# Splitting the branch weights ahead of the first gate product in three merges of a two-layer diffusion block

## The chip, the cores and the metric

The kernel runs on one core of a Trainium2 chip. The metric is device time in microseconds (us), median of several executions. A profile is one execution with the hardware profiler; its rows are quoted below. PE is TensorE, DVE is VectorE, ACT is ScalarE, POOL is GpSimd, SP the queue that issues most transfers.

## What is computed

Two layers over 256 latent tokens (x) and, in layer 0 only, 256 context tokens as well. Each layer has a normalised input projection, three parallel mixers (attention, convolution, pooling), a merge of them with gates, and then 16 routed experts whose weights are streamed from memory. The part that matters here:

```
y_a = attn @ w_attn_o;  y_b = conv(..) @ w_conv_o;  y_c = pool(..) @ w_pool_o
g_a, g_b, g_c = split(sigmoid(gate_in), 3)          # gate_in: 3 x 1024 columns of h @ w_in
out = (g_a * y_a + g_b * y_b + g_c * y_c) @ w_out
```

## The kernel before

**Split products.** Every product of the layer body is made of three fast products. `split` (L229 to L240) turns 128x1024 weights into a high half, written by ACT (L238), and a low half, the weights minus the high half, written by DVE or POOL (L239). Both halves go into one tile `ws`. `mm3` then multiplies: first the high half with both halves of the activations (L496 and L497 in turn, two for each of `nk` blocks), then the low half with the high activations (L499, one for each block). So a product can start when ACT is done, and needs the low half only two thirds later. Which engine makes the low half is in the table `LOW`: a letter for each layer, v for DVE and p for POOL (`g0="vv"`, `g1="pv"`, `g2="vp"`, `wo="vv"`).

**The `ws` buffers.** Tiles `ws` come from a pool with two buffers. In layer 1 (`last`), every third split takes a third buffer of its own (pool `DR`). A tile is released when its last reader is done. The framework has a scheduler that orders the instructions of each engine at build time, by a priority that follows the order of the code and by when a buffer comes free; `split` lifts its two instructions ahead by a fixed amount (`SPLIT_PRIO`). On the chip each engine works through its own list in order.

**A merge.** `merge(bi, w_o, brt)` runs three times in each layer: branch 0 (attention, L763), branch 2 (pooling, L811), branch 1 (convolution, L820). It walks four column blocks q. A q has two steps v. A step has a gate product (`unit`, called u0 or u1 here by its v: 24 matmuls against `hh`, `hl`), a tanh on ACT, and a branch product (p0, p1: 12 matmuls against `br`, `brp` or `brc`), which DVE then multiplies with the gate; POOL adds it to the sum in branches 2 and 1 (L761). The gate weights of u0 and u1 are split apart (called g0 and g1 here); the branch weights are split once for both steps of a q (called wo here). In layer 0 a matmul has 512 columns, in layer 1 it has 256.

**What else is woven in.** The convolution's taps (L478) run on DVE under the first merge. `pump_mod` puts 4 modulation products (L255, for the next stage) behind a unit, `mod_group` ends with `modr` on DVE (L264), transposes (L271) and one product (L294). The scheduler may move all of these. Weight tiles `w` come through a ring of five buffers filled by SP.

Of the kernel before, what the change touches and what calls it, by code (L numbers as in the profile page):

```python
# [27 lines left out]
LOW = dict(q="vv", k="pv", v="pv", cg="vv", ca="vv", pu="pv", g0="vv", g1="pv", g2="vp", wo="vv", wout="pv")  # L28
# [99 lines left out]
def dit_block(ctx: ExitStack, tc: tile.TileContext, out, kcv, kb16, rope_in, tok, cols, w_mod0, w_mod,  # L128
# [16 lines left out]
    def bank(tag, dt=F32):  # L145
        pool, bufs = psum[tag]
        return pool.tile([128, 512], dt, tag=tag, name=tag, bufs=bufs)
# [19 lines left out]
    def t2(name, n=512, dt=F32):  # L167
        return L.tile([128, n], dt, tag="t2", name=name, bufs=6)
# [42 lines left out]
    for l in range(DEPTH):  # L211
# [10 lines left out]
        def load(src, view, **kw):  # L222
            t = ring()
            nc.sync.dma_start(t, src)
            return t.rearrange(view, **kw)
# [3 lines left out]
        def split(src, view, eng="v", **kw):  # L229
            nsplit[0] += 1  # L230
            if last and nsplit[0] % 3 == 0 and not tail[0]:
                w = DR.tile([128, 2048], F32R, tag="ws", name="ws")
            else:
                w = LW["pool"].tile([128, 2048], F32R, tag="ws", name="ws", bufs=2)
            hi, lo = w[:, :1024], w[:, 1024:]
            h, lw = hi.rearrange(view, **kw), lo.rearrange(view, **kw)
            with tc.high_priority(SPLIT_PRIO[l]):
                nc.scalar.activation(h, src, AF.Copy)  # L238
                (nc.gpsimd if eng == "p" else nc.vector).tensor_sub(lw, src, h.bitcast(F32))  # L239
            return hi, lo  # L240
# [126 lines left out]
        for s in range(2):  # L367
# [8 lines left out]
            for t in range(2):  # L376
                nc.vector.tensor_scalar(xn[s][:, t, :], XS[s][:, t, :], r[:, t:t + 1],
                                        None, op0=ALU.mult)
# [91 lines left out]
        def pump_taps(n):  # L470
            for _ in range(min(n, len(taps))):
                ch, k = taps.popleft()
                if k == 0:
                    nc.vector.tensor_scalar(acc[:, ch], up[:, ch, :, 0:256], dw[:, ch:ch + 1],
                                            vec[:, VCB + 4 * l + ch:VCB + 4 * l + ch + 1],
                                            op0=ALU.mult, op1=ALU.add)
                else:
                    nc.vector.scalar_tensor_tensor(acc[:, ch], up[:, ch, :, k:k + 256],  # L478
                                                   dw[:, 4 * k + ch:4 * k + ch + 1], acc[:, ch],
                                                   op0=ALU.mult, op1=ALU.add)  # L480
# [11 lines left out]
        def mm3(ps, w, a, nk, n):  # L492

            (wh, wl), (ah, al) = w, a
            for k in range(nk):
                nc.tensor.matmul(ps, wh[:, k, :], ah[:, k, :n], start=k == 0, stop=False)  # L496
                nc.tensor.matmul(ps, wh[:, k, :], al[:, k, :n], start=False, stop=False)  # L497
            for k in range(nk):
                nc.tensor.matmul(ps, wl[:, k, :], ah[:, k, :n], start=False, stop=k == nk - 1)  # L499

        def unit(src, n, view="p (k n) -> p k n", eng="v", **kw):
            w = split(src, view, eng, **(kw or dict(k=8)))
            w = [v.rearrange("p (k n) -> p k n", k=8) for v in w]
            ps = bank("mm")
            mm3(ps[:, :n], w, (hh, hl), 8, n)
            nunit[0] += 1
            if nunit[0] % MOD_EVERY[l] == 0:
                pump_mod()
            return ps

        def win(c0):
            return load(w_in[l, c0 // 256], "p (k n) -> p k n", k=8)
# [224 lines left out]
        def merge(bi, w_o, brt, fill=None):  # L737
            for q in range(4):
                if q % 2 == 0:
                    wo = load(w_o[l, q // 2], "p (k n) -> p k n", k=4)  # L740
                wgt = win(OGATE + 1024 * bi + 256 * q)
                ws = None
                for v in range(2):
                    j = 2 * q + v
                    pg = unit(wgt[:, :, 128 * v:128 * v + 128], N, eng=LOW[f"g{bi}"][l])
                    th = t2("th", N)
                    nc.scalar.activation(th, pg[:, :N], AF.Tanh, scale=0.5)
                    if ws is None:
                        ws = split(wo[:, :, 256 * (q % 2):256 * (q % 2) + 256], "p (k n) -> p k n",
                                   LOW["wo"][l], k=4)  # L750
                        ws = [z.rearrange("p (k n) -> p k n", k=4) for z in ws]
                    py = bank("mm")
                    mm3(py[:, :N], [z[:, :, 128 * v:128 * v + 128] for z in ws],
                        (brt[:, 0], brt[:, 1]), 4, N)
                    if bi == 0:
                        nc.vector.scalar_tensor_tensor(m[j], th, 1.0, py[:, :N], op0=ALU.add,
                                                       op1=ALU.mult)
                    else:
                        nc.vector.scalar_tensor_tensor(th, th, 1.0, py[:, :N], op0=ALU.add,
                                                       op1=ALU.mult)  # L760
                        nc.gpsimd.tensor_add(m[j], m[j], th)  # L761
                    pump_taps(TAPS.get(f"merge{bi}", (0, 0))[l])
                    if fill is not None and not taps:  # L763
                        next(fill, None)

        merge(0, w_attn_o, br)

        brp = branch("brp")
# [40 lines left out]

        cn = conv_norm()  # L810
        merge(2, w_pool_o, brp, cn)  # L811
        pump_taps(len(taps))
        for _ in cn:
            pass
        brc = branch("brc")
        for ch in range(4):
            z = acc[:, ch].rearrange("p s n -> p (s n)")
            nc.scalar.activation(brc[:, 0, ch, :], z, AF.Copy)
            nc.vector.tensor_sub(brc[:, 1, ch, :], z, brc[:, 0, ch, :].bitcast(F32))
        merge(1, w_conv_o, brc)  # L820
        pump_mod(100)

# [210 lines left out]
        for e in range(NE):  # L1033
# [36 lines left out]
            for i in range(4):  # L1070
                wg, wu = [eload().rearrange("p (k n) -> p k n", k=2) for _ in range(2)]
                for kk in range(2):
                    k = 2 * i + kk
# [126 lines left out]
```

## Time and profile before

| | us |
|---|---|
| median of 3 executions | 1696.55 (1694.93 to 1698.94) |
| the profiled execution | 1699.61 |
| its span, first to last instruction | 1697.8 |

PE is busy for 1469.8 us, 87% of the span; DVE for 40%, ACT for 24%, POOL for 14%. By time, the merges of layer 0 take 201 to 425 us, those of layer 1 take 1080 to 1205 us, and the experts follow each. A row of a timeline gives start, length, engine, line, operation, output and input, then in brackets how long the engine was idle before it and what ended that. The ends of matmuls are modelled, so the distance of two starts is the better measure of a matmul.

### The profile page before, as it was taken

Reading aid. Unit: us, or ns where it says so; the run is one execution under the profiler, and the core shown is the slowest. Engines: PE = TensorE matmul, PEld = TensorE weight load, DVE = VectorE, ACT = ScalarE, POOL = GpSimd, SP = SyncE. Lnnn points to the kernel's source line nnn. Section 1 sums busy time; section 2 is a strip of 40 time slices with the busy share of each in tenths; the row PEclk is TensorE's granted clock in tenths of the full one; section 3 lists DMA queues with packets and bytes.
Section 4 is the critical chain, followed back from the end, with each engine's and each line's share of the span. In section 5 each row is a group of like instructions: output and inputs, shape, how many; then the busy total and the mean of one; then the engine's idle time right before and its main releaser. Section 6 shows DMA issues by size and latency. Waiting matters only on the chain.

```text
span 1697.8 us, 19127 instructions
## 1 busy us (share of the span) xinstructions
PE 1469.8 (87%) x7788; PEld 797.6 (47%) x7788; DVE 673.0 (40%) x1141; ACT 407.1 (24%) x760; POOL 231.1 (14%) x234
## 2 busy tenths in 40 slices
PE   6999989999899999999988899999978656666575
PEld 2666667888654433333332377789843111111111
DVE  3589983441652221121211378966532110111011
ACT  3466212232432100100000258334421000000001
POOL 0301610254730000000000020225100000000000
PEclk9999999999999999999999999999989886887878
DMA  9644445243447999999999765665699999999995
GB/s 398 235 174 140 142 172 180 99 184 138 173 177 302 428 425 428 428 426 428 428 426 427 304 239 184 220 251 202 248 387 428 427 428 428 428 427 428 428 428 240
DMA packets 48185, 530.01 MB, mean 312 GB/s; under 512 B 5345, under 2 KB 6113, under 8 KB 7906
## 3 DMA queue, kind: packets, MB, share of 16 engines
q1 hardware_dynamic: 46224, 526.10, 76.2%
q10 hardware_dynamic: 1874, 2.70, 0.5%
q8 instruction: 61, 1.00, 0.2%
q14 instruction: 26, 0.21, 0.0%
HBM read 527.73 MB, written 1.05 MB: 311 GB/s over the span
## 4 chain that ended last, share of the span: by engine, by line
PE 38%; DMA 27%; DVE 4%; issue 2%; ACT 1%; POOL 1%; POOLq 0%; ACTq 0%; DVEq 0%; SPq 0%
DMA we<-in_w_e_dram 24%; PE mm L1080 11%; PE mm L1103 6%; PE mm L987 3%; PE mm L872 3%; PE mm L497 2%; PE mm L496 2%; PE mm L499 2%; DMA A<-in_w_e_dram 2%; PE ax L1125 2%; DVE acc L478 1%; PE mm L1108 1%; PE ax L1095 1%; PE md L255 1%; DVE ws L239 1%
## 5 line engine op out<-in xcount | busy, mean ns | idle before, releaser
L1080 PE MATMUL mm<-we,xeT 128*32 128x512 f32 (+1 forms) x1880 | 348.0, 662 | 99.5 <-DMA we<-in_w_e_dram 99.5
L1080 PEld LDWEIGHTS mm<-we,xeT 128*32 128x32 f32 (+1 forms) x1880 | 94.8, 129 | 342.2 <-issue 186.6
L496 PE MATMUL mm<-hh,ws 128*128 128x512 f32 (+1 forms) x672 | 222.8, 350 | 0.2
L497 PE MATMUL mm<-hl,ws 128*128 128x512 f32 (+1 forms) x672 | 219.7, 345 | 0.8 <-DVE hl L430 0.8
L238 ACT ACTIVATE ws<-w 128x1024 fp32r<-128x1024 f32 x132 | 139.4, 1058 | 301.0 <-PE mm L499 192.8
L1087 DVE TENSOR_TENSOR hm<-si,mm 64x512 f32<-64x512 f32 x48 | 33.1, 690 | 413.0 <-ACT si L1085 272.3
L1085 ACT ACTIVATE si<-mm 64x512 f32<-64x512 f32 x48 | 28.3, 590 | 686.7 <-PE mm L1080 686.7
L478 DVE SCALAR_TENSOR_TENSOR acc<-up,dw,acc 128x512 f32<-128x512 f32 (+1 forms) x240 | 154.5, 685 | 1.1
L239 DVE TENSOR_TENSOR ws<-w,ws 128x1024 fp32r<-128x1024 f32 x94 | 124.6, 1329 | 66.9 <-ACT ws L238 66.4
L496 PEld LDWEIGHTS mm<-hh,ws 128*128 128x128 f32 x672 | 128.3, 192 | 28.9 <-issue 12.6
L497 PEld LDWEIGHTS mm<-hl,ws 128*128 128x128 f32 x672 | 128.2, 191 | 18.6 <-issue 3.5
L499 PE MATMUL mm<-hh,ws 128*128 128x512 f32 (+1 forms) x672 | 132.5, 339 | 0.7 <-DVE ws L239 0.6
L239 POOL TENSOR_TENSOR ws<-w,ws 128x1024 fp32r<-128x1024 f32 x38 | 95.8, 2527 | 203.6 <-ACT ws L238 124.3
L1103 PE MATMUL mm<-we,hT 128*64 128x512 f32 x432 | 111.0, 637 | 4.8 <-ACT hT L1098 4.8
L499 PEld LDWEIGHTS mm<-hh,ws 128*128 128x128 f32 x672 | 107.2, 189 | 15.2 <-DVE ws L239 1.4
L1045 POOL COPY sel<-kc 48x128 f32<-48x128 f32 (+1 forms) x16 | 4.6, 285 | 798.2 <-DVE hm L1087 427.3
L1115 DVE TENSOR_TENSOR Y<-mm,G 32x512 f32<-32x512 f32 x64 | 44.0, 687 | 132.3 <-PE mm L1103 131.5
L1108 PE MATMUL mm<-we,hT 128*32 128x512 f32 x424 | 70.2, 779 | 9.4 <-DMA we<-in_w_e_dram 6.3
L1103 PEld LDWEIGHTS mm<-we,hT 128*64 128x64 f32 x432 | 33.6, 146 | 76.0 <-issue 65.3
L1125 PE MATMUL ax<-Y,sg 128*128 128x512 f32 x128 | 58.4, 603 | 8.8 <-DVE Y L1118 6.4
L1095 PE MATMUL ax<-kc,hm 64*128 64x64 f32 x192 | 32.6, 295 | 30.9 <-DVE hm L1087 30.2
L1118 DVE TENSOR_TENSOR Y<-mm,G 64x512 f32<-64x512 f32 x32 | 22.0, 689 | 94.0 <-PE mm L1108 93.6
(261 smaller groups left out, 1708.0 us busy)
## 6 DMA issues: line engine op xcount, KB each, us to landing
we<-in_w_e_dram SPq DMA_DIRECT2D x166, 2048.0 KB, 27.1
w<-in_w_mod_dram SPq DMA_DIRECT2D x44, 1024.0 KB, 5.4
w<-in_w_in_dram SPq DMA_DIRECT2D x42, 1024.0 KB, 4.8
A<-in_w_e_dram SPq DMA_DIRECT2D x20, 2048.0 KB, 23.8
w<-in_w_out_dram SPq DMA_DIRECT2D x12, 1024.0 KB, 4.9
we<-in_w_e_dram SPq DMA_DIRECT2D x10, 1024.0 KB, 17.2
wm<-in_w_mod_dram SPq DMA_DIRECT2D x4, 1024.0 KB, 19.1
w<-in_w_attn_o_dram SPq DMA_DIRECT2D x4, 1024.0 KB, 4.8
```

The lines of the kernel that those rows point to most:

```text
L238: nc.scalar.activation(h, src, AF.Copy)
L239: (nc.gpsimd if eng == "p" else nc.vector).tensor_sub(lw, src, h.bitcast(F32))
L478: nc.vector.scalar_tensor_tensor(acc[:, ch], up[:, ch, :, k:k + 256], dw[:, 4 * k + ch:4 * k + ch + 1], acc[:, ch], op0=ALU.mult, op1=ALU.add)
L496: nc.tensor.matmul(ps, wh[:, k, :], ah[:, k, :n], start=k == 0, stop=False)
L497: nc.tensor.matmul(ps, wh[:, k, :], al[:, k, :n], start=False, stop=False)
L499: nc.tensor.matmul(ps, wl[:, k, :], ah[:, k, :n], start=False, stop=k == nk - 1)
L872: nc.tensor.matmul(pss[t], a, b, start=k == 0 and st == 0, stop=k == 7 and st == 2)
L987: nc.tensor.matmul(px, XS[s][:, t, paired(d)], Sv, start=t == 0, stop=t == 1)
L1080: nc.tensor.matmul(o, xeT[k // 4][:, k % 4, e, :], w[:, kk, 512 * f:512 * f + 512], start=k == 0, stop=k == 7)
L1103: nc.tensor.matmul(pd[64 * h:64 * h + 64, :], hT[:, 64 * k:64 * k + 64], rhs, start=k == 0, stop=k == 7)
L1108: nc.tensor.matmul(pd[o:o + 32, :], hT[:, c0:c0 + 32], rhs, start=k < 2, stop=k >= 6)
L1125: nc.tensor.matmul(po, sgs[s][:, t * 128:(t + 1) * 128], Y[:, s, cols], start=True, stop=True)
```

## The change

The split of wo moves ahead of the loop over v, so it is issued before g0 is split and not behind the first gate product.

```diff
                 wgt = win(OGATE + 1024 * bi + 256 * q)
-                ws = None
+                ws = split(wo[:, :, 256 * (q % 2):256 * (q % 2) + 256], "p (k n) -> p k n",
+                           LOW["wo"][l], k=4)
+                ws = [z.rearrange("p (k n) -> p k n", k=4) for z in ws]
                 for v in range(2):
                     j = 2 * q + v
                     pg = unit(wgt[:, :, 128 * v:128 * v + 128], N, eng=LOW[f"g{bi}"][l])
                     th = t2("th", N)
                     nc.scalar.activation(th, pg[:, :N], AF.Tanh, scale=0.5)
-                    if ws is None:
-                        ws = split(wo[:, :, 256 * (q % 2):256 * (q % 2) + 256], "p (k n) -> p k n",
-                                   LOW["wo"][l], k=4)
-                        ws = [z.rearrange("p (k n) -> p k n", k=4) for z in ws]
                     py = bank("mm")
```

The count of instructions and bytes stays. What moves is which buffer a split takes, and with it what it waits for. In the built programs the buffers (A, B, and D for the third one of layer 1) go over two q, where a stroke marks the next q, like this:

| | g0 | wo | g1 | g0' | wo' | g1' |
|---|---|---|---|---|---|---|
| layer 0 before | A | B | A | A | B | A |
| layer 0 after | B | A | B | A | B | A |
| layer 1 before | A | B | D | A | B | D |
| layer 1 after | B | A | D | A | B | D |

Before, g0' takes the buffer that u1 (layer 0) or u0 (layer 1) left, and wo' takes the one that p1 leaves. After it, wo' asks first and takes the buffer that is free earlier, and g0' takes the one that p1 leaves.

**First place: PE at the start of the first merge in layer 0.** `ws_1654` is the last pooling unit. Before, `ws_1709` is g0 and `ws_1766` is wo:

```order
L499 MATMUL mm_1657<-hh_116,ws_1654 128x512 x8
L496 MATMUL mm_1712<-hh_116,ws_1709 128x512
...
L499 MATMUL mm_1712<-hh_116,ws_1709 128x512 x8
L271 MATMUL ax_1737<-kc_71,modr_1682 128x128 x4
L294 MATMUL ax_1751<-modr_1682,gsel_1746 128x512
L255 MATMUL md_1755<-w_1756,cst_79 32x512 x4
L496 MATMUL mm_1769<-br_625,ws_1766 128x512
```

After, `ws_1712` is g0 and `ws_1709` is wo:

```order
L499 MATMUL mm_1657<-hh_116,ws_1654 128x512 x8
L271 MATMUL ax_1740<-kc_71,modr_1682 128x128 x4
L294 MATMUL ax_1754<-modr_1682,gsel_1749 128x512
L496 MATMUL mm_1715<-hh_116,ws_1712 128x512
L497 MATMUL mm_1715<-hl_117,ws_1712 128x512
```

The transposes of `modr` and the product behind them moved from behind u0 to ahead of it. On DVE the list is the same up to and with `modr` (L264); the next low half behind it was that of wo and is now that of g0, behind as many taps.

**Second place: ACT in the last merge of layer 0.** The rows run from wo of q = 0 into q = 1. Before, `ws_2864` is g0', `ws_2894` wo' and `ws_2912` g1':

```order
L238 ACTIVATE ws_2817<-w_2767 128x1024
L747 ACTIVATE th_2797<-mm_2772 128x512
L238 ACTIVATE ws_2864<-w_2862 128x1024
L747 ACTIVATE th_2845<-mm_2820 128x512
L238 ACTIVATE ws_2894<-w_2765 128x1024
L238 ACTIVATE ws_2912<-w_2862 128x1024
```

After, `ws_2864` is wo' and `ws_2867` is g0':

```order
L238 ACTIVATE ws_2817<-w_2767 128x1024
L749 ACTIVATE th_2800<-mm_2775 128x512
L238 ACTIVATE ws_2864<-w_2765 128x1024
L749 ACTIVATE th_2845<-mm_2820 128x512
L238 ACTIVATE ws_2867<-w_2862 128x1024
L238 ACTIVATE ws_2912<-w_2862 128x1024
```

The two high halves changed places: g0' is the one behind p1 now. PE's own list in this merge is u0, p0, u1, p1, u0' with nothing between, before and after.

**Third place: POOL in the second merge of layer 1**, where POOL makes the low halves of the gates. Before, `ws_7092` and `ws_7158` are g0 and g1 of q = 0, `ws_7229` and `ws_7295` those of q = 1:

```order
L239 TENSOR_TENSOR ws_7092<-w_7090,ws_7092 128x1024
L239 TENSOR_TENSOR ws_7158<-w_7090,ws_7158 128x1024
L239 TENSOR_TENSOR ws_7229<-w_7227,ws_7229 128x1024
L761 TENSOR_TENSOR A_61<-A_61,th_7120 128x256
L239 TENSOR_TENSOR ws_7295<-w_7227,ws_7295 128x1024
L761 TENSOR_TENSOR A_61<-A_61,th_7192 128x256
```

After, `ws_7158` is g1 and `ws_7095` g0 of q = 0, `ws_7295` is g1 and `ws_7232` g0 of q = 1:

```order
L239 TENSOR_TENSOR ws_7158<-w_7090,ws_7158 128x1024
L239 TENSOR_TENSOR ws_7095<-w_7090,ws_7095 128x1024
L759 TENSOR_TENSOR A_61<-A_61,th_7123 128x256
L239 TENSOR_TENSOR ws_7295<-w_7227,ws_7295 128x1024
L759 TENSOR_TENSOR A_61<-A_61,th_7192 128x256
L239 TENSOR_TENSOR ws_7232<-w_7227,ws_7232 128x1024
```

g1, whose own buffer comes free with the u1 before, now stands ahead of g0 of the same q, and so does the addition of the last step.

## Rows read from the trace of the kernel before

**Rows 1.** Busy by stretch: length; PE, PEld, DVE, ACT, POOL; PEclk; DMA share, GB/s.

```profile
364.00:424.00 60.00, 60.00 (x266) 49.70 (x265) 13.09 (x13) 15.95 (x20) 26.63 (x16) 1.00 0.51 193
...
550.00:650.00 100.00, 95.64 (x442) 38.79 (x438) 23.24 (x38) 11.54 (x22) 0.57 (x2) 0.97 1.01 427
...
1300.00:1400.00 100.00, 64.22 (x399) 16.58 (x400) 14.73 (x22) 4.66 (x10) 0.57 (x2) 0.86 1.01 428
```

**Rows 2.** Waits of PE in layer 1's merges: total, times, longest.

```profile
PE mm L499 <- DVE ws L239: 3.0, 2, 2.4
PE mm L497 <- DVE brp L774: 1.2, 1, 1.2
```

**Rows 3.** Timeline of the start of layer 0's first merge, PE and DVE.

```profile
201.63 0.39 PE L496 MATMUL mm<-hh,ws 128*128 128x512 f32 x1
...
205.93 0.68 DVE L264 TENSOR_TENSOR modr<-md,modb 128x512 f32<-128x512 f32 x1
206.06 2.12 PE L499 MATMUL mm<-hh,ws 128*128 128x512 f32 x8 [0.64 <-DVE ws L239]
...
208.02 0.63 PE L271 MATMUL ax<-kc,modr 128*128 128x128 f32 x4
...
209.44 1.07 PE L255 MATMUL md<-w,cst 128*32 128x512 f32 x8
...
215.51 1.22 DVE L239 TENSOR_TENSOR ws<-w,ws 128x1024 fp32r<-128x1024 f32 x1
...
216.78 2.08 PE L499 MATMUL mm<-br,ws 128*128 128x512 f32 x4 [4.25 <-DVE ws L239]
...
226.22 1.06 PE L255 MATMUL md<-w,cst 128*32 128x512 f32 x8
```

**Rows 4.** PE alone by stretch: length, busy (count), granted clock, DMA share, GB/s.

```profile
217.00:220.00 3.00, 3.00 (x8) 0.50 0.00 0
...
431.00:435.00 4.00, 2.60 (x10) 1.00 0.59 207
...
1097.00:1099.00 2.00, 2.00 (x10) 0.50 1.01 418
...
1128.00:1132.00 4.00, 2.83 (x20) 1.00 0.79 262
```

**Rows 5.** Timeline of layer 0's last merge, from one q into the next.

```profile
383.72 0.39 PE L496 MATMUL mm<-hh,ws 128*128 128x512 f32 x1
...
389.41 1.06 ACT L238 ACTIVATE ws<-w 128x1024 fp32r<-128x1024 f32 x1 [6.61 <-issue]
...
390.55 2.40 POOL L239 TENSOR_TENSOR ws<-w,ws 128x1024 fp32r<-128x1024 f32 x1 [4.50 <-ACT ws L238]
...
391.88 0.39 PE L496 MATMUL mm<-hh,ws 128*128 128x512 f32 x1
...
392.08 1.07 ACT L238 ACTIVATE ws<-w 128x1024 fp32r<-128x1024 f32 x1 [1.12 <-PE mm L499]
```

**Rows 6.** Timeline of layer 1's first merge at the start of its second q.

```profile
1090.05 0.36 PE L496 MATMUL mm<-hh,ws 128*128 128x256 f32 x1
...
1095.59 1.22 DVE L239 TENSOR_TENSOR ws<-w,ws 128x1024 fp32r<-128x1024 f32 x1
...
1096.86 1.23 PE L499 MATMUL mm<-br,ws 128*128 128x256 f32 x4 [2.40 <-DVE ws L239]
```

**Rows 7.** Timeline of layer 1's second and last merge, POOL and PE.

```profile
1145.79 4.79 POOL L239 TENSOR_TENSOR ws<-w,ws 128x1024 fp32r<-128x1024 f32 x2 [2.65 <-ACT ws L238]
...
1152.30 1.03 PE L783 MATMUL ax<-kc,acc 128*128 128x128 f32 x8
...
1154.54 0.73 POOL L761 TENSOR_TENSOR A<-A,th 128x256 f32<-128x256 f32 x1
...
1187.48 0.28 PE L496 MATMUL mm<-hh,ws 128*128 128x256 f32 x1
...
1191.80 0.28 PE L496 MATMUL mm<-hh,ws 128*128 128x256 f32 x1
```

## The prediction

> **What bounds the kernel now.** I first read busy time by stretch. In the last merge of layer 0, PE is busy 60.00 of 60 us at clock 1.00 while DMA is busy for 0.51 [rows 1]; in the expert stretches DMA is at 1.01 in both layers. So the merges are bound by PE, and the expert stream that follows them by the transfers. The second does not cushion the first: expert weights go into buffers that the merges and the projection behind them hold, so a merge that ends later starts the stream later, and I let a slip of PE in a merge through to the end in full.
>
> Next come the waits of PE inside the merges, since a moved split can only take away or add such waits. There is little to win. Layer 1 has 3.0 us for low halves from DVE, 2.4 of it in one wait, and 1.2 us for `brp` [rows 2]. Layer 0 has 0.64 and 4.25 us at its first merge [rows 3] and nothing in the later stretch of [rows 1].
>
> Then the clock. After the 4.25 us wait the granted clock was 0.50, the lower level of 1.2 GHz, and likewise after the 2.40 us one; it stayed at 1.00 around waits of about 1 us (431 to 435 and 1128 to 1132 us) [rows 4]. The cost of the low level is read from [rows 3]: from 216.78 to 226.22, 9.44 us, PE does 4 matmuls of p0 and 24 of u1. At full clock a step of 36 takes 391.88 - 383.72 = 8.16 us [rows 5], 0.227 each, so these 28 would take 6.4. The slow phase costs 3.1 us.
>
> **The change part by part.** No instruction is added or removed; PE work, bytes and transfers are those of before. SP's list keeps its order. The whole effect is which buffer a split takes, and so what it waits for, and where the scheduler then puts things.
>
> *A gate split behind p1.* Before, g0' was split while p1 ran, since its buffer was free: the ACT row at 389.41 comes 2.5 us ahead of the product at 391.88 [rows 5]. It was wo' that waited for p1, at 392.08, and a whole unit of 5.45 us lay between it and its reader. After the change g0' waits there, and its reader is the next instruction of PE. The price is from the same rows: ACT starts 0.20 us behind the point where PE would go on, takes 1.07, and I add 0.05 for the signal, as between the end of the low half (215.51 + 1.22) and PE at 216.78 [rows 3]. That is 1.3 us at a bare boundary. PE's order says which are bare. In layer 0 the first merge has 5 modulation products there (4 take 1.0 us, as from 226.22 on, so 1.25: covered), the step into the second merge has four products of `dz` (covered), and the second merge has 10, 10 and 12 transposes at about 0.1 us each [rows 7], which leaves 0.5 in all. Bare are the step into the last merge and three inside it: 4 x 1.3 = 5.2. Sum 5.7 us; at least 4.2 with the ACT time alone, at most 7. The low half of POOL does not add to it: an addition and 2.40 us fit in front of the 16 matmuls (3.6 us) ahead of its reader.
>
> In layer 1 the last merge has three bare boundaries, and one that is half covered by four transposes: 3.9 + 0.8, less 0.4 for a `brc` wait that a later PE no longer sees: 4.3 us (3.4 to 5.5).
>
> *POOL in layer 1's second merge.* Here the low halves of both gates are POOL's, at 4.79 / 2 = 2.40 us, and the additions take 0.73 [rows 7]. A step is shorter: 1191.80 - 1187.48 = 4.32 us for 36 matmuls, 0.12 each, so u is 2.88, p 1.44, and the low half is wanted 1.92 us after u starts. Count from the end of u1. g1' has its own buffer and is split at once: ACT done at 1.2, POOL at 3.6. The addition of p0 goes to 4.3. Only then g0': to 6.7. PE ends p1 at 1.44, has 1.25 to 1.8 us of moved products, starts u0' near 2.7 to 3.2 and wants the low half at 4.6 to 5.1. So PE waits about 1.45, 1.6 and 1.85 us at the first three q. At the fourth nothing covers ACT (1.6 with the tanh ahead of it), and one more multiplication of 0.7 stands before POOL's low half: 1.6 + 2.55. Sum 9.1, and 1.0 for a clock that falls once. Against it stand the waits of before that go: 1.2 for `brp`, 0.6 for a low half [rows 2] and some 0.8 of slow going around them, 2.6. Net 7.5 us; 3.7 if the additions find room elsewhere, 10 if the clock falls at each wait.
>
> *Start of layer 0's first merge.* PE now meets the transposes of `modr` ahead of u0. `modr` ends at 205.93 + 0.68 = 206.6, and DVE's list up to there is unchanged, while PE is free at 201.63: a wait of about 5 us that u0 used to fill. Transposes and product take 209.44 - 208.02 = 1.4, so u0 starts at 208.1, and its high part ends 3.6 later at 211.7. Its low half now stands where that of wo stood on DVE, behind as many taps, at 215.51 + 1.22 = 216.7 [rows 3]. From there 8 matmuls of u0 (1.8), 4 modulation products (1.0), p0 (2.7) and u1 (5.45) end at 227.7, against 226.22: +1.5, or +4.6 with the slow phase of 3.1 that followed a wait of this kind. I take 4.0, since two long waits come in a row.
>
> *Start of layer 1's first merge.* The low half that PE waited for, done at 1096.8 [rows 6], was that of wo', wanted at 1094.5. DVE's list is the same in length there, and this place is now that of g0'. u0' starts near 1091.0, behind five modulation products, and wants it at 1092.9: a wait of 4.2 for 2.4. The products pulled forward are no loss. With the slow phase I take +2.0 (0.3 to 3).
>
> The sum is 5.7 + 4.3 + 7.5 + 4.0 + 2.0 = 23.5 us. The profiled execution would go from 1699.61 to 1723.1; it lies 3.1 above the median, so the median goes from 1696.55 to **1720.0 us**. The low ends give 4.2 + 3.4 + 3.7 + 1.5 + 0.3 = 13.1, the high ends 7 + 5.5 + 10 + 4.6 + 3 = 30.1: 1710 to 1727.
>
> **The rivals.**
>
> *The clock falls at the short gaps too.* There are about 12 gaps of 1.3 us or more where PE ran through. For it: PE is at 0.50 after each of the two long waits. Against it: 1.00 around the waits of about 1 us, one of them with PE busy for only 2.60 of 4 us [rows 4]. If each gap cost a slow phase of 0.9 (ten matmuls of layer 1 at half rate) to 3.1 us, 11 to 35 us would come on top: 1731 to 1755. The Trainium skill, "TensorE: Matmul & The Clock Gate", section "A second HAM failure mode: psum-queue depth-cycling", tells of a kernel in which PE idled briefly and often between groups of matmuls and so had its clock go to and fro. By that rule this rival is the case; the trace so far shows the low level behind the long waits alone. Chance 0.14.
>
> *The early split pays.* The gain would lie at the two starts of the first merges: wo is ready before p0 asks, so the wait of 4.25 with its 3.1 of slow phase, and the 2.4 with some 1.0, go: 1696.55 - 10.8 = 1686. It decides at the low half of g0: DVE would have to end it by 211.7 and not 216.7. Against it, the same taps stand ahead of it in DVE's list, and `modr` in front of u0 costs 5 us before that. Chance 0.04.
>
> *Nothing to see.* ACT is busy for 13.09 of 60 us [rows 1], and the scheduler moved products into half of the boundaries. If the bare ones were covered as well, and POOL kept pace, only the small ends of the two starts were left: 0 to 3 us, 1697 to 1700. Against it, PE's order has nothing between p1 and u0' in the last merges, and the buffer can't be written before p1 has read it. Chance 0.05.
>
> **How the numbers follow.** The forecast has 0.77, the rivals 0.14, 0.04 and 0.05. The likeliest one's own range is 1710 to 1727. For 8 in 10 I take **1706 to 1735 us**, which adds the lower part of the clock rival and some room for places where the scheduler's new order of taps makes PE wait less. A change of less than 0.2%, 3.4 us, can't be told from none in this kernel. Faster by more has 0.04, within it 0.05, slower 0.91.
>
> **What would show it.** PE should have about eight waits of 1.1 to 1.4 us for a high half from ACT (`ws`, L238) in 359 to 435 and 1165 to 1225 us, none before. A wait of 4 to 5 us of the transposes for `modr` near 202 to 207 us, and one of 2 to 5 us for a low half from DVE near 217. Waits of the low-half products for POOL in layer 1's second merge, four of 1.4 to 2.6 us. The experts' stretches keep their lengths. I am wrong if the ACT row of g0' starts before p1 has ended, if POOL's low half of g0' comes ahead of that of g1', if the granted clock is at 0.50 after 1.3 us gaps, or if the expert stretches get shorter and take the slip back.

## The result, and the profile after

The changed kernel takes 1725.3 us (median of 4 executions, 1724.2 to 1728.1); the kernel before, run beside it, took 1697.7 (4 executions, 1694.9 to 1700.2). The ratio is 1.0161, 95% interval 1.0146 to 1.0176: slower by about 27 us, where 23.5 were forecast. The profiled execution took 1724.2 us with a span of 1722.0, which is 24.2 more than the span before.

Busy time by stretch, as in [rows 1], first: length; PE, PEld, DVE, ACT, POOL; granted clock; DMA share, GB/s.

```profile
364.00:424.00 60.00, 55.41 (x240) 44.32 (x239) 15.65 (x15) 16.63 (x22) 27.74 (x17) 1.00 0.46 175
550.00:650.00 100.00, 97.04 (x456) 38.98 (x454) 24.59 (x40) 9.75 (x19) 0.57 (x2) 0.98 0.99 417
1300.00:1400.00 100.00, 75.12 (x484) 25.75 (x484) 19.39 (x32) 8.31 (x18) 0.57 (x2) 0.86 1.01 428
```

In layer 0's last merge PE was busy for 60.00 of 60 us [rows 1]; now it idles for 4.6 of them, at a clock of 1.00 as before. The expert stretches are still bound by the transfers. What PE waits for is in the waits of PE (total, times, longest), first those from 359 to 440 us, then from 1085 to 1230:

```profile
PE mm L496 <- ACT ws L238: 4.6, 4, 1.1
...
PE mm L496 <- ACT ws L238: 5.3, 5, 1.2
PE mm L499 <- POOL ws L239: 4.9, 4, 2.6
PE mm L499 <- DVE ws L239: 3.0, 1, 3.0
```

The kernel before had no wait in the first stretch up to the end of its last merge at 425.8 us. In the second, [rows 2] had 3.0 us for DVE and 1.2 for `brp`, and nothing for ACT or POOL. The timeline of the changed kernel shows each kind of wait once:

```profile
207.07 0.68 DVE L264 TENSOR_TENSOR modr<-md,modb 128x512 f32<-128x512 f32 x1
207.80 1.13 PE L271 MATMUL ax<-kc,modr 128*128 128x128 f32 x4 [4.87 <-DVE modr L264]
209.65 1.42 PE L496 MATMUL mm<-hh,ws 128*128 128x512 f32 x1
216.94 1.22 DVE L239 TENSOR_TENSOR ws<-w,ws 128x1024 fp32r<-128x1024 f32 x1
218.22 2.09 PE L499 MATMUL mm<-hh,ws 128*128 128x512 f32 x8 [2.49 <-DVE ws L239]
229.63 1.07 PE L255 MATMUL md<-w,cst 128*32 128x512 f32 x8
233.58 1.90 PE L255 MATMUL md<-w,cst 128*32 128x512 f32 x10
233.68 1.06 ACT L238 ACTIVATE ws<-w 128x1024 fp32r<-128x1024 f32 x1 [2.40 <-PE mm L499]
235.41 0.50 PE L496 MATMUL mm<-hh,ws 128*128 128x512 f32 x1
249.28 1.06 PE L255 MATMUL md<-w,cst 128*32 128x512 f32 x6
...
383.14 1.07 PE L499 MATMUL mm<-brc,ws 128*128 128x512 f32 x4
384.25 1.06 ACT L238 ACTIVATE ws<-w 128x1024 fp32r<-128x1024 f32 x1 [1.12 <-PE mm L499]
385.36 0.50 PE L496 MATMUL mm<-hh,ws 128*128 128x512 f32 x1 [1.15 <-ACT ws L238]
...
403.12 0.50 PE L496 MATMUL mm<-hh,ws 128*128 128x512 f32 x1 [1.15 <-ACT ws L238]
...
1154.12 1.22 PE L499 MATMUL mm<-hh,ws 128*128 128x256 f32 x8 [0.17 <-POOL ws L239]
...
1177.06 2.38 POOL L239 TENSOR_TENSOR ws<-w,ws 128x1024 fp32r<-128x1024 f32 x1
1179.49 2.08 PE L499 MATMUL mm<-hh,ws 128*128 128x256 f32 x8 [2.64 <-POOL ws L239]
```

The rows from 383 to 403 answer to [rows 5]. The branch product p1 issues its last matmuls from 383.14 on; ACT begins the next gate's high half at 384.25, ends at 385.31, and the gate product starts at 385.36, with 1.15 us of idle PE ahead of it. A step of this merge is 403.12 - 385.36 = 17.76 us long, where [rows 5] have 8.16 from one gate product to the other within a step, and two of these make 16.32.

### The profile page after: what moved, and what is told of

It reads as the page before. It is cut to its first block, busy times and chain, and to the rows that moved or that the text cites. A ratio compares the mean times of both kernels' runs of the same rounds, so it can differ in the third digit from the quotient of the medians.

```text
span 1722.0 us, 19129 instructions
## 1 busy us (share of the span) xinstructions
PE 1474.4 (86%) x7788; PEld 798.7 (46%) x7788; DVE 669.3 (39%) x1141; ACT 406.1 (24%) x760; POOL 227.2 (13%) x234
## 5 line engine op out<-in xcount | busy, mean ns | idle before, releaser
L1078 PE MATMUL mm<-we,xeT 128*32 128x512 f32 (+1 forms) x1880 | 345.3, 657 | 97.1 <-DMA we<-in_w_e_dram 96.8
L239 DVE TENSOR_TENSOR ws<-w,ws 128x1024 fp32r<-128x1024 f32 x94 | 118.2, 1259 | 115.4 <-ACT ws L238 114.9
L478 DVE SCALAR_TENSOR_TENSOR acc<-up,dw,acc 128x512 f32<-128x512 f32 (+1 forms) x240 | 150.0, 667 | 1.0
L759 POOL TENSOR_TENSOR A<-A,th 128x512 f32<-128x512 f32 (+1 forms) x32 | 35.6, 1111 | 194.1 <-DVE th L757 194.1
```

Source lines behind the costliest of these rows:

```text
L1078: nc.tensor.matmul(o, xeT[k // 4][:, k % 4, e, :], w[:, kk, 512 * f:512 * f + 512], start=k == 0, stop=k == 7)
```

## The experiments

To compare them I cut each trace at the same work: the unit ahead of the first merge, `dz` behind it, and in each merge the first matmul of its first gate product u0, then the first matmul of the projection. Lengths in us:

| kernel | layer 0: first | second | last | layer 1: first | second | last |
|---|---|---|---|---|---|---|
| before | 90.35 | 72.84 | 66.60 | 45.57 | 42.63 | 37.89 |
| changed | 95.22 | 74.94 | 71.31 | 48.12 | 49.93 | 40.87 |
| mid | 89.68 | 72.85 | 66.59 | 45.57 | 42.44 | 37.89 |
| own2 | 96.80 | 73.70 | 67.61 | 48.48 | 45.50 | 37.91 |
| m1 | 89.65 | 74.15 | 71.29 | 45.60 | 45.80 | 40.86 |
| g2dve | 96.77 | 74.94 | 71.29 | 49.32 | 42.49 | 40.85 |
| nostart | 93.34 | 74.94 | 71.31 | 46.71 | 49.89 | 40.87 |
| own2_g2 | 96.75 | 73.70 | 67.60 | 48.40 | 39.68 | 37.90 |
| bown1 | 89.04 | 73.68 | 67.61 | 44.68 | 46.66 | 37.89 |
| b_g2dve | 89.67 | 72.85 | 66.59 | 45.54 | 39.92 | 37.89 |
| b_g2dve again | 89.68 | 72.85 | 66.59 | 44.13 | 39.92 | 37.93 |
| best_own0 | 89.66 | 72.84 | 66.59 | 45.28 | 39.92 | 37.90 |
| cut53 | 91.38 | 72.84 | 66.59 | 44.59 | 42.07 | 37.92 |

(The "second" columns hold the step into the last merge.) Each row is one execution. The first merges vary most from one execution to the next: b_g2dve, traced twice, gave 45.54 and 44.13 us in layer 1, and in layer 0 the 90.35 of the kernel before stands against 89.65 to 89.68 in the four traces with the same work there (m1, b_g2dve twice, best_own0). A difference of 1.4 us in a first merge of layer 1, or of 0.7 in one of layer 0, is therefore not yet an effect.

Theory 1 is that of the prediction: what costs is the buffer that the branch weights take, and what the scheduler then moves. The main rival is that an earlier split costs by itself, by its place in the lists of ACT and VectorE.

**mid: the split early, the buffers as before.**

```diff
-        def unit(src, n, view="p (k n) -> p k n", eng="v", **kw):
+        def unit(src, n, view="p (k n) -> p k n", eng="v", then=None, **kw):
             w = split(src, view, eng, **(kw or dict(k=8)))
+            if then is not None:
+                then()
...
-                    pg = unit(wgt[:, :, 128 * v:128 * v + 128], N, eng=LOW[f"g{bi}"][l])
+                    pg = unit(wgt[:, :, 128 * v:128 * v + 128], N, eng=LOW[f"g{bi}"][l], then=wsplit)
```

(`wsplit` makes the branch split the first time that it is called in a step.)

> The kernel before with the branch weights' split issued right behind the split of the step's first gate weights, still ahead of the first gate product: earlier than before, but the gate's split takes the buffer that came free first, as before. Theory 1 (the cost is the buffer: the branch weights take the one freed early and the next gate split waits for the end of the branch product): nothing of that is left, so about 1698 us, within 4 of the kernel before, and no row of about 1.15 us in which PE waits for ACT at a step of layer 0's last merge. Rival 2 (an earlier split of the branch weights crowds ACT and VectorE whatever buffer it takes): 1715 to 1726.

Measured: 1698.6 us, ratio 1.0003 (0.9991 to 1.0015). Its waits of PE from 200 to 436 us hold no ACT:

```profile
PE mm L499 <- DVE ws L239: 5.2, 3, 4.2
PE mm L877 <- POOL ws L239: 1.0, 1, 1.0
PE mm L877 <- DVE ml L832: 0.8, 1, 0.8
```

Every length in the table is that of before within 0.7 us. Issued ahead of the gate product but behind the gate's split, the branch split costs nothing. In the program the only difference to the changed kernel is which of the two splits comes first, so first choice of the buffer and first place in the lists are still one thing here.

**own2: the order of the change, with buffers of their own.**

```diff
+            if own == 0:
+                hi = DR.tile([128, 1024], F32R, tag="KS", name="ws")
+                lo = DR.tile([128, 1024], F32R, tag="KL", name="ws")
+            elif own == 1:
+                w = DR.tile([128, 2048], F32R, tag="qf", name="ws")
...
-                           LOW["wo"][l], k=4)
+                           LOW["wo"][l], own=q % 2 if bi else None, k=4)
```

> The changed kernel, in which the branch weights of the second and last merges of both layers get two buffers of their own, where keys and queries of the attention lay (8 KB each); the first merges stay as changed. Theory 1 (buffer): the waits at the step boundaries of these merges go, in layer 0 some 0.8 + 6 to 7 us, in layer 1 some 7 + 3 us, so 1708 us (1704 to 1712), and the four waits of 1.15 us for ACT in layer 0's last merge are gone. Rival 2 (the order on ACT, VectorE and POOL costs it, not the buffer): 1720 to 1727. Rival 3 (the tensor clock falls at the gaps): as theory 1 in time, but then the granted clock of these merges would be higher than in the changed kernel, where it is 1.00 already.

Measured: 1711.7 us, ratio 1.0063 (1.0041 to 1.0085), 13.6 us less than the changed kernel by the medians, 16.6 by the ratios. In its timeline of layer 0's last merge

```profile
382.77 1.09 PE L506 MATMUL mm<-brc,ws 128*128 128x512 f32 x4
382.97 1.06 ACT L245 ACTIVATE ws<-w 128x1024 fp32r<-128x1024 f32 x1 [0.27 <-PE mm L504]
383.70 0.40 PE L503 MATMUL mm<-hh,ws 128*128 128x512 f32 x1
```

the gate product at 383.70 waits for nobody: what ACT writes at 382.97 is for later. (The gate splits of these merges then have all the other buffers to themselves.) With the same early order in the program, the last merges lose 3.7 and 3.0 us of their excess and the second ones 1.2 and 4.4. So the buffer is what costs, and the rival of the order falls for these merges. Two remainders: a step in layer 0 takes 16.6 us for 16.32, matmul for matmul a little longer, in bown1 too; I did not follow why. And 2.9 us stay in layer 1's second merge, which own2_g2 takes up.

**m1: the change in the last merges alone.**

```diff
+                if bi == 1:
+                    ws = split(wo[:, :, 256 * (q % 2):256 * (q % 2) + 256], "p (k n) -> p k n",
+                               LOW["wo"][l], k=4)
+                    ws = [z.rearrange("p (k n) -> p k n", k=4) for z in ws]
```

> The change in the last merges alone (both layers); the first and the second merges as in the kernel before. Theory 1 with the terms as the changed kernel's trace has them: layer 0 four boundaries at 1.5 us, 6 us, and layer 1 some 3 to 4 us: 1698 + 9.5 = 1707 us (1705 to 1710). If the terms were not separate (what the last merge loses depends on what the earlier ones lost): under 1703 or over 1712.

Measured: 1710.3 us, ratio 1.0068 (1.0049 to 1.0087), 11.5 us; by the table 1.3 + 4.7 in layer 0 and 3.2 + 3.0 in layer 1, 12.1. This is at the upper edge of what was expected. Of the 3.2, 1.3 is the step into layer 1's last merge, which belongs to the change as well; 1.8 lie in the first step of the second merge, whose splits stand as in the kernel before: PE waits 1.92 us for `brp` there, for 1.17 in the kernel before, and the granted clock behind it (1136 to 1140 us) is 0.57. The last merges have the same lengths as in the changed kernel (71.29 and 40.86), so the terms are separate.

**g2dve, b_g2dve and own2_g2: where POOL comes in.** One edit, put into the changed kernel, the kernel before and own2:

```diff
-LOW = dict(q="vv", k="pv", v="pv", cg="vv", ca="vv", pu="pv", g0="vv", g1="pv", g2="vp", wo="vv", wout="pv")
+LOW = dict(q="vv", k="pv", v="pv", cg="vv", ca="vv", pu="pv", g0="vv", g1="pv", g2="vv", wo="vv", wout="pv")
```

> The changed kernel, with the low half of layer 1's second merge's gate weights subtracted on VectorE and not on POOL. Theory 1 with POOL's own term (the late gate split waits on POOL behind the sums of the merge): the 4.9 us of waits for POOL go and some come back on VectorE: 1721 us (1719 to 1723). Rival (POOL is only where the late buffer shows): the same wait moves to VectorE or ACT, 1724 to 1727.

Measured: 1718.4 us, ratio 1.0112 (1.0097 to 1.0127), 7 us off the changed kernel, more than expected. From 1092 to 1226 us PE no longer waits for POOL, and the wait did not move to another engine:

```profile
PE mm L496 <- ACT ws L238: 5.3, 5, 1.2
PE mm L499 <- DVE ws L239: 3.0, 1, 3.0
```

The second merge goes from 49.93 to 42.49. Before I booked that as the cost of the change on POOL, the same edit had to go into the kernel before:

> The kernel before with the same edit as the one that gave 1718.4 in the changed kernel: the low half of layer 1's second merge's gate weights on VectorE and not on POOL. Theory 1 (POOL's place in the chain costs something only where the gate split is late): within 3 us of 1698. Rival (POOL's subtraction is a loss in either order, and the 7 us were no part of the change): 1690 to 1693.

Measured: 1694.9 us, ratio 0.9973 (0.9961 to 0.9985). It lies between the two expectations. POOL's low halves cost 42.63 - 39.92 = 2.7 us in the old order too, and 7.4 in the new. The traces show what the 2.7 are. DVE and POOL in the kernel before, then DVE in b_g2dve:

```profile
1119.39 8.67 DVE L478 SCALAR_TENSOR_TENSOR acc<-up,dw,acc 128x256 f32<-128x256 f32 x9
1122.58 5.20 POOL L239 TENSOR_TENSOR ws<-w,ws 128x1024 fp32r<-128x1024 f32 x2 [36.17 <-ACT ws L238]
1148.40 3.26 DVE L239 TENSOR_TENSOR ws<-w,ws 128x1024 fp32r<-128x1024 f32 x1 [0.60 <-ACT ws L238]
...
1119.59 3.08 DVE L478 SCALAR_TENSOR_TENSOR acc<-up,dw,acc 128x256 f32<-128x256 f32 x6
```

A tap takes 0.48 us here, but the two that DVE runs under POOL's two subtractions take 2.49 and 2.51, and a low half of DVE's own that falls under a later one takes 3.26 us for 1.22. What DVE ends late is what PE waits for: `brp` (1.17 us) and that low half (0.60). The two branch products with these waits take 3.31 us (1128.54 to 1131.85) and 2.31 (1149.99 to 1152.30) where 12 matmuls at 0.12 take 1.44, which makes the 2.7. With no subtraction on POOL in this merge, the taps are back at 0.48 (six in 3.08) and both waits are gone.

> The changed kernel with both edits: own buffers for the branch weights of the second and last merges, and the low halves of layer 1's second merge on VectorE. If POOL's 7 us consist of some 4.7 that the late buffer makes and 2.7 that POOL costs in either order: the edit is worth 2 to 3 us here, 1709 us. If POOL's cost is one thing and independent of the buffer: 7 us, 1704 to 1705.

Measured: 1703.2 us, ratio 1.0024 (1.0014 to 1.0035). The merge goes from 45.50 to 39.68, 5.8 us, neither the 2.7 nor the 7.4. The subtraction on POOL costs something else in each order, and it is not a sum of a late buffer and a fixed loss. In own2 it is DVE once more:

```profile
1130.54 9.10 DVE L485 SCALAR_TENSOR_TENSOR acc<-up,dw,acc 128x256 f32<-128x256 f32 x7
1134.37 7.48 POOL L246 TENSOR_TENSOR ws<-w,ws 128x1024 fp32r<-128x1024 f32 x3 [2.16 <-PE mm L506]
```

Three of the seven taps take 1.96 to 2.52 us, PE waits 3.06 for `brp`, and the granted clock from 1139 to 1147 us is 0.57; own2_g2 has no such tap and no such wait. The changed kernel has no stretched tap either: its taps are done before POOL starts at 1137.17, and what PE waits for there is POOL itself (4.9 us). What does hold: with own buffers and VectorE this merge takes 39.68, as in b_g2dve (39.92), so nothing of the early split is left there; with late buffers and VectorE 2.6 are left.

**nostart: the change without the first step of the first merge.**

```diff
+                if bi or q:
+                    ws = split(wo[:, :, 256 * (q % 2):256 * (q % 2) + 256], "p (k n) -> p k n",
+                               LOW["wo"][l], k=4)
+                    ws = [z.rearrange("p (k n) -> p k n", k=4) for z in ws]
```

> The changed kernel, in which only the first step of the first merge (each layer) splits as the kernel before does. Theory 1 (the first merge's start is a term of its own, 2.3 us in layer 0 by the changed trace: PE waits 4.87 for VectorE's modr, then 2.49 for the low half): about 1725.5 less 2 to 4, 1721.5 to 1723.5, and the wait for modr is gone. Rival (the start is made up later, since the merge runs into other waits anyway): 1725 to 1727. If the lower clock that follows the wait (0.50 in the slices from 207 to 212) costs as much again: under 1720.

Measured: 1721.7 us, ratio 1.0123 (1.0106 to 1.0140), 3.6 us less than the changed kernel by the medians, 6.5 by the ratios. The wait for `modr` is gone. In layer 0 the first merge goes from 95.22 to 93.34. In layer 1 it goes from 48.12 to 46.71, but PE's wait there is 2.99 us in both; the granted clock behind it is 1.00 here and 0.60 in the changed kernel, so these 1.4 us are the clock and not shown to be the edit. Of what stays in layer 0, 3.0 us over 90.35, the boundaries of this merge, for which the prediction had nothing, are 3 x 0.86 = 2.6; the next experiment is on these.

**cut53: the kernel before, modulation products in fives and threes.** In the changed kernel's timeline above, five modulation products (ten rows, L255) stand at 233.58 and take until 235.41, 1.83 us, though ACT was done at 233.68 + 1.06 = 234.74; three (six rows) at 249.28 take 1.0, as long as four (eight rows, 229.63 to 230.62). In the kernel before they always come in fours.

```diff
                 for j in range(4):
                     nc.tensor.matmul(ps[32 * j:32 * j + 32, :],
                                      cst[:, k].rearrange("p s m -> p (s m)"),
                                      w[:, j * 512:(j + 1) * 512], start=k == 0, stop=k == 7)
+                    if (4 * k + j) % 8 == 4:
+                        yield
                 w = wn
-                yield
+                if k % 2:
+                    yield
```

> The kernel before with nothing moved but the cut of the modulation products: TensorE gets them in turns of five and three, where it got four and four. The prediction's term of zero (products that stand at a boundary only cover a wait): 1698 us, within 4. The reading of the changed trace (four products run side by side, a fifth costs 0.85 us alone, and the three cost as much as four): some 12 pairs in layer 0 and 5 in layer 1, those behind other waits free: 8 to 14 us, 1706 to 1712.

Measured: 1703.7 us, ratio 1.0025 (1.0013 to 1.0036): slower, so not the prediction's zero, but by 4 and not by 8 to 14. The timeline of layer 0's first merge:

```profile
253.88 0.39 PE L499 MATMUL mm<-hh,ws 128*128 128x512 f32 x1
259.41 1.91 PE L255 MATMUL md<-w,cst 128*32 128x512 f32 x10
269.67 1.06 PE L255 MATMUL md<-w,cst 128*32 128x512 f32 x6
273.52 0.39 PE L499 MATMUL mm<-hh,ws 128*128 128x512 f32 x1
293.17 1.02 PE L774 MATMUL ax<-dz,wp 128*128 128x512 f32 x2
```

The starts of u0 in the kernel before, then in the changed kernel:

```profile
248.84 0.39 PE L496 MATMUL mm<-hh,ws 128*128 128x512 f32 x1
267.62 0.39 PE L496 MATMUL mm<-hh,ws 128*128 128x512 f32 x1
...
255.05 0.50 PE L496 MATMUL mm<-hh,ws 128*128 128x512 f32 x1
274.69 0.50 PE L496 MATMUL mm<-hh,ws 128*128 128x512 f32 x1
```

Two steps of cut53 take 273.52 - 253.88 = 19.64 and 19.65 us. In the kernel before they take 18.78 (248.84, 267.62 and `dz` at 286.40), in the changed kernel 19.64 (235.41, 255.05, 274.69). The cut alone makes the 0.86 us per step, in the old order of the splits. It does so where PE runs through. Up to layer 0's `dz` the kernel lost 6.8 us, 5.7 of them ahead of its first merge; in this merge as a whole it lost only 1.0 (91.38 for 90.35), since its waits are 1.8 us at most and its granted clock stays at 1.00. In layer 1, where I had counted five pairs, it lost nothing.

**bown1 and best_own0: is there a gain in more buffers?** bown1 is the kernel before with `own=0` for all branch splits, in the old order; best_own0 is b_g2dve with `own=0` in layer 1's first merge alone.

> The kernel before, in its own order, with one buffer more: the branch weights' halves lie in the 8 KB of the attention's keys, so that gate splits wait for no branch product. Theory 1 (in layer 1's merges PE waits 8.0 us for the low halves, part of it because the buffers come free late): 1693 to 1697. Rival (there the splits are bound by ACT and VectorE themselves): 1697 to 1700.

Measured: 1700.0 us, ratio 1.0003 (0.9992 to 1.0013). The 8.0 us that the expectation starts from are not in the kernel before: its waits for low halves in layer 1's merges are 3.0 us [rows 2]. The wait of 2.4 us in layer 1's first merge goes, with one of 2.2 us for an `A` of DVE in its place; 44.68 for 45.57 is within the spread of that column. The second merge takes 46.66 for 42.63: two taps and a low half of DVE are stretched under POOL (2.50, 2.48 and 3.04 us), and PE waits 3.7 us for `brp`. The rival had the time right, the reason is another.

> The kernel before with the low halves of layer 1's second merge on VectorE, and besides, in layer 1's first merge alone, the branch weights in the 8 KB of the attention's keys. The one wait for a low half that is left in layer 1's merges is 2.4 us, in this merge; with the buffer the merge took 0.9 us less. If the gain adds: 1 us under the kernel without the buffer, 1693 to 1695; rival (other waits take it up): the same as that kernel, 1695.

> The kernel before with the low halves of layer 1's second merge on VectorE, once more, in five rounds: the first three gave 1694.9 us, 0.27% under the kernel before, and its trace 2.7 us less in this merge. If that is real: a ratio of 0.9965 to 0.9990; if it was the run's spread: 1.000.

Measured: best_own0 1694.9 us, ratio 0.9972 (0.9961 to 0.9982); b_g2dve again 1694.7, ratio 0.9973 (0.9961 to 0.9984). The buffer adds nothing. The low halves on DVE alone beat the kernel before by 0.27%, twice. This is the best version here, and it has nothing to do with the change.

## Why the prediction was right, and where its terms were off

The direction and the mechanism held, the time was 5 us above the forecast and inside the range. By term, from the profiled pair:

| term | forecast | measured | from |
|---|---|---|---|
| layer 0, start of the first merge | 4.0 | 2.3 (3.8 elsewhere) | 226.22 to 229.63, less 1.14 that was there before the merges |
| layer 0, first merge's boundaries | 0 | 2.6 | three at 0.86 |
| layer 0, second merge | 0.5 | 0.8 | 2.10 in the table, less the step into the last merge |
| layer 0, last merge | 5.2 | 6.0 | 4.71 and 1.3 for the step into it |
| layer 1, first merge | 2.0 | 2.55 | table |
| layer 1, second merge | 7.5 | 6.0 | 7.30 in the table, less 1.30 for the step into the last merge |
| layer 1, last merge | 4.3 | 4.3 | 2.98 in the table and 1.30 for the step into it |
| sum | 23.5 | 24.5 | span: 24.2 |

*A gate split behind p1.* The step held to a tenth: ACT started 0.20 us behind the point where PE would have gone on, and took 1.06; PE followed 0.05 later. In the length of a step there are 17.76 - 16.32 = 1.44 and not 1.3, since the first matmul behind the wait takes 0.34 to the next and not 0.23: its weight load stands at 385.36 as well, and not ahead of it as with the others (385.70 for 385.93). Four waits of 1.15 stand in layer 0, as the section on what would show it has them. mid and own2 tie this to the buffer.

*"The first merge has 5 modulation products there (4 take 1.0 us, as from 226.22 on, so 1.25: covered)".* This is the step that failed. Five take 1.83, and the three that are left still take 1.0, so the cover itself cost 0.86 per step. cut53 shows it without any wait.

*Start of layer 1's first merge.* The time is right (2.55 for 2.0), the reason is not, and that is luck. The wait was to grow from 2.4 to 4.2 us; it grew to 2.99: u0' starts 0.7 us later than forecast and needs 2.2 us, not 1.9, up to its low half. "The products pulled forward are no loss" does not hold: before, four groups of four take 4.0 us in this merge; now groups of four, five, seven and five take 0.99, 1.84, 1.85 and 1.83, which is 6.5. How much of these 2.5 us would have been waits anyway was not tested in layer 1. The two executions whose clock did not fall there, nostart and b_g2dve again, differ by 46.71 - 44.13 = 2.58 as well.

*Start of layer 0's first merge.* The wait for `modr` came as told (4.87 for about 5), and the low half ended at 218.16, against the forecast of 216.7: 1.14 by which this execution was already late ahead of the merge, and 0.3. But the clock did otherwise. Granted clock of PE alone, by stretch:

```profile
207.00:212.00 5.00, 4.20 (x10) 0.50 0.02 3
212.00:217.00 5.00, 3.73 (x13) 0.85 0.00 0
217.00:220.00 3.00, 1.78 (x8) 1.00 0.00 0
...
382.00:387.00 5.00, 3.85 (x17) 1.00 1.06 452
...
1107.00:1111.00 4.00, 2.98 (x14) 0.60 0.99 418
...
1179.00:1184.00 5.00, 4.51 (x25) 0.66 0.57 210
...
1208.00:1213.00 5.00, 3.85 (x32) 1.00 0.16 29
```

The slow phase followed the first wait and lay on the high half of u0, which would have had to wait for its low half anyway; behind the second wait the clock was 1.00. In three of the experiments that have the same work up to there (own2, g2dve, own2_g2) it came back behind the second wait: the granted clock from 217 to 220 us was 0.63, 0.68 and 0.68, the 8 low matmuls took 3.3 to 3.7 us for 2.09, and the first merge is 96.8 us long for 95.2. There the term is 3.8, or 4.5 when the kernel before is taken at the 89.7 us of the four other traces. The forecast of 4.0 was fair; the profiled execution was a lucky one, which is also a part of why the pair gives 24.2 and the medians 27.

*POOL in layer 1's second merge.* The mechanism held and the size was 1.5 us too high. PE waited for POOL 0.58, 0.17 and 1.52 us at the first three steps, where 1.45, 1.6 and 1.85 were forecast, and 1.23 (ACT) and 2.64 at the fourth (1.6 and 2.55): 6.1 for 9.1. What stands ahead of u0' takes 1.83, 2.99 and 1.84 us at the first three and not 1.25 to 1.8, so u0' starts later and the wait is shorter: what was missed as a cost was missed here as a cover. The clock fell once in this merge, behind the 2.64, as booked; from 1179.49 to 1183.49 the 20 matmuls at 0.12 lost 1.6 us, for 1.0. The waits of before that went are 1.17 and 0.60, 1.8 for 2.6 with the slow going. 6.1 + 1.6 - 1.8 makes 5.9, and 6.0 were measured. POOL's queue in the order low half, sum, low half was seen as told.

*The last merge of layer 1.* The forecast counted the step into it, and with this step the sum of 4.3 is met. That step cost 1.30 for 0.8; in it are the four transposes of `modr`, 0.48 us that stood inside the merge before. Of the three boundaries inside, two cost 1.41 and 1.40, and the first only 0.06 net: the transposes have left its step, and the wait for `brc`, and the mixed order that went with it, are gone. That compensation was booked at 0.4 and is about 1.3.

*No cushion.* The expert stretches kept their lengths, but the time between the two layers' merges moves by itself: the slip of 12.8 us at the end of layer 0's merges was 11.2 at the start of layer 1's, and in the experiments it shrank by up to 3.1 or grew by up to 1.8 on this way. I take that as the spread of the transfers; it was not tested.

*The rivals.* The clock stays at 1.00 around the gaps of 1.15 us in both last merges (the rows at 382 and 1208), and falls in this kernel behind waits of 2.64, 2.99 and 4.87 only. So the costly rival did not come about. The kernel of which the Trainium skill tells on "TensorE: Matmul & The Clock Gate", section "A second HAM failure mode: psum-queue depth-cycling", idles briefly and often and has its clock go to and fro; nine waits for ACT, most of 1.15 us, some 18 us apart in layer 0 and 10 in layer 1, did not do that here. The early split did not pay: the low half of g0 ended at 218.16, less 1.14 for the late start 217.0, which is 5.3 us behind the 211.7 by which it would have.

## What to carry to other kernels

When two buffers turn over among several users, moving an allocation moves a wait: look for who now takes the buffer that comes free late, and how many instructions stand between that write and its reader (one unit of 5.45 us before, none after). Ask for the same split behind the more urgent one, as in mid, and it costs nothing. A suspect that gives a gain in the changed kernel has to be tried in the kernel before as well: moving POOL's subtractions was worth 7.4 us in the one and 2.7 in the other, through other waits, and the 2.7 are the only gain of this study. Work that is given to POOL to spare DVE has to be looked at on DVE's own rows: here it made DVE's taps five times as long.

## What the chip did that I had not expected

Four products of 32 columns run side by side and take about 1.0 us together; a fifth takes 0.84 more, and three take as long as four (1.83 us for five, 0.98 for three, 0.99 for four). The Trainium skill, on "TensorEngine Tiling (Array Packing)", has a division of the array into four tiles of 128 x 32 (section "Available Configurations") and says that tiles run matmuls in parallel (section "Key Properties"). Three or four at the price of one agree with that; the price of a group cut in two is what these traces add.

The low clock does not follow the same wait of the same program each time. b_g2dve, traced twice, waits 2.40 us for the same low half in layer 1's first merge both times. PE alone behind it, first trace and second:

```profile
1096.00:1100.00 4.00, 3.88 (x20) 0.58 1.01 414
...
1096.00:1100.00 4.00, 4.00 (x36) 1.00 1.00 406
```

The merge took 45.54 and 44.13 us. Behind the second wait of layer 0's first merge the clock was 1.00 in one execution and 0.63 to 0.68 in three others with the same work up to there, which moved this merge by 1.5 us.

A DVE instruction that runs under a subtraction of POOL can take five times as long: taps of 2.49 and 2.51 us for 0.48 in the kernel before, and a low half of 3.26 for 1.22. `brp` on DVE, whose input comes from PE's result `ax`, was not stretched (1.65 us for four, under POOL's subtraction in own2, as in the kernel before).
